# Four pieces for one: splitting GpSimd's 128x2048 subtractions in a three-layer transformer kernel

## The chip, the cores and the metric

The kernel runs on one NeuronCore of a Trainium2 chip. Its time is the device time of one execution in microseconds. The engines have one queue of instructions each: TensorE (PE in the profile, PEld for its weight loads), VectorE (DVE), ScalarE (ACT), GpSimd (POOL) and SyncE (SP, which here issues most of the loads). They wait for one another by semaphores.

## The reference

Three layers work on one sequence of 256 tokens with 1024 features, all in float32:

```
layers 0, 1:  h = rms_norm(x) * (1 + sc1) + sh1          # sh, sc, g from silu(c) @ ada_w
              x = x + g1 * attention(h @ w_qkv) @ w_o    # layer 0 differential, layer 1 banded with a relative bias
              h = rms_norm(x) * (1 + sc2) + sh2
              x = x + g2 * moe(h)                        # 16 experts, two per token
layer 2:      the same frame; p = h @ w_in feeds a gated mlp, attention over tokens and context,
              and a two-way gated scan; then @ w_out and an moe with 32 experts, two per token
```

## The kernel before, in words

Tokens lie in two tiles of 128 partitions (`NT = 2`). The dense weights (`w_qkv`, `w_o`, `w_in`, `w_out`) come in slabs of 128 partitions x 4 x 512 float32, 1 MB each, through `stream` (L231). SP loads a slab `w` (L243). `split` (L246) makes two float32r tiles of it: `hi`, a rounded copy (`copy`, L250 by way of L188, mostly on ACT), and `lo = w - hi` (`tt`, L251 by way of L199). The second is the operation at issue. A table (`ENG`, entries `sv0` and `sv1`, L142 and L143) and a default say whether it runs on DVE or GpSimd: 30 of these subtractions are on GpSimd, 16 on DVE.

`mm3` (L265) then multiplies in three passes: rounded activations by `hi`, the activations' low part by `hi`, and rounded activations by `lo`. So a slab's `lo` is wanted 16 matmuls later than its `hi`. `trans_split` (L482 to L199) makes the activations' own two parts at the start of a layer: `affine` on ACT (L519) and DVE (L521), and a 128x512 subtraction on DVE (L199).

All slabs, loads and large activations share one pool of 17 buffers named `u`. SP issues loads in program order and waits in the queue until the buffer is free; a slab is free when its subtraction has read it.

Small DVE work that stands beside the subtractions: `rsqrt` (L284), a chain of tiny operations, each needing the one before (L288, L289, then three times L295 or L297 and L298, and L299), for the norms of a layer (results used at L464) and of the queries and keys (used at L199, and then by TensorE's transposes at L573); `coef` (L452), the eight numbers per partition with which the layer's activations are scaled; and `ada_close` (L422), which ends a modulation vector.

The order of the steps in a mix stage is a string (`MIX_ORDER`), and the framework's scheduler sets the order within each engine's queue when the program is built. Between the mix stages stand the experts' stages (L1646 to L1716), whose weights are used unsplit; they have a 128x512 subtraction of their own on GpSimd (L1682). Before each expert stage all engines meet at a branch (L1725, L1726).

Of the kernel before, what the change touches and what calls it, by code (L numbers as in the profile page):

```python
# [9 lines left out]
F32 = mybir.dt.float32  # L10
# [3 lines left out]
OP = mybir.AluOpType  # L14
# [106 lines left out]
SPV = 3  # L121
# [44 lines left out]
class Gen:  # L166
# [64 lines left out]
    def stream(self, srcs, raw):  # L231


        srcs, loaded, ready = list(srcs), [], []
        n = [0]

        def load(m):
            while srcs and len(loaded) < m:
                src = srcs.pop(0)
                w = self.t("u", [128, 4, 512])  # L240
                n_ = 4 // len(src)
                for i, q in enumerate(src):
                    self.nc.sync.dma_start(w[:, i * n_:(i + 1) * n_], q)  # L243
                loaded.append(w)

        def split():  # L246
            w = loaded.pop(0)
            hi, lo = (self.t("u", list(w.shape), F32R) for _ in range(2))

            self.copy("sh", hi, w)  # L250
            self.tt("sv", lo, w, hi.bitcast(F32), OP.subtract, "VG" if n[0] % SPV == SPV - 1 else "GV")  # L251
            n[0] += 1
            ready.append((hi, lo))

        def get():
            load(raw)
            while loaded and len(ready) < 2:
                split()
                load(raw)
            return ready.pop(0)  # L260

        get.load, get.split = load, split
        return get
# [1625 lines left out]
```

## Time and profile before

| | |
|---|---|
| three runs | 1600.05, 1605.42, 1606.1 us; median 1605.42 |
| the profiled execution | 1605.76 us, of which 1603.9 us from its first to its last instruction |
| PE busy | 1448.1 us (90%), 7202 matmuls |
| DVE busy | 642.9 us (40%) |
| ACT busy | 405.2 us (25%) |
| POOL busy | 255.8 us (16%), 126 instructions |
| mean granted TensorE clock | 0.956 of full speed |
| HBM | 336 GB/s over the span |

The shares are averages over stages of two kinds. In the experts' stages the DMA engines are busy throughout (most slices at 410 to 423 GB/s in the page's strip) and GpSimd is nearly idle. The mix stages, at about 30 to 215, 440 to 660 and 900 to 1140 us, hold all the 128x2048 subtractions. There the DMA share is lower in most slices, and DVE's digit reaches 9.

### The profile page before, as it was taken

Reading aid. Unit: us, or ns where it says so; the run is one execution under the profiler, and the core shown is the slowest. Engines: PE = TensorE matmul, PEld = TensorE weight load, DVE = VectorE, ACT = ScalarE, POOL = GpSimd, SP = SyncE. Lnnn points to the kernel's source line nnn. Section 1 sums busy time; section 2 is a strip of 40 time slices with the busy share of each in tenths; the row PEclk is TensorE's granted clock in tenths of the full one; section 3 lists DMA queues with packets and bytes.
Section 4 is the critical chain, followed back from the end, with each engine's and each line's share of the span. In section 5 each row is a group of like instructions: output and inputs, shape, how many; then the busy total and the mean of one; then the engine's idle time right before and its main releaser. Section 6 shows DMA issues by size and latency. Waiting matters only on the chain. (4 is left out here: it accounts for less than half of the span.)

```text
span 1603.9 us, 18619 instructions
## 1 busy us (share of the span) xinstructions
PE 1448.1 (90%) x7202; PEld 768.5 (48%) x7202; DVE 642.9 (40%) x1404; ACT 405.2 (25%) x717; POOL 255.8 (16%) x126
## 2 busy tenths in 40 slices
PE   4999989999979988899999798678899999999997
PEld 1666643454356566444534265456435445434432
DVE  3678521221176675242122458976113122212212
ACT  1455211011054443132111255532111111101100
POOL 1332201101032412001000233321010100100100
PEclk8999979999989989999999899889899999999999
DMA  9787859999979937499999657318699999999997
GB/s 363 276 319 272 331 215 423 421 421 421 410 282 364 340 132 314 175 416 416 421 418 416 226 189 261 130 46 322 245 421 421 421 421 421 421 422 420 421 421 294
DMA packets 131071, 540.86 MB, mean 337 GB/s; under 512 B 8600, under 2 KB 13856, under 8 KB 83360
## 3 DMA queue, kind: packets, MB, share of 16 engines
q1 hardware_dynamic: 128032, 533.73, 83.9%
q10 hardware_dynamic: 2320, 3.89, 0.7%
q0 software_dynamic: 624, 1.98, 0.3%
q8 instruction: 60, 0.98, 0.2%
q14 instruction: 35, 0.29, 0.0%
HBM read 538.49 MB, written 1.06 MB: 336 GB/s over the span
## 5 line engine op out<-in xcount | busy, mean ns | idle before, releaser
L1646 PE MATMUL ps<-u,b 128*64 128x512 f32 x2048 | 487.9, 601 | 14.1 <-DMA u<-in_w_dram 10.2
L1646 PEld LDWEIGHTS ps<-u,b 128*64 128x64 f32 x2048 | 166.3, 138 | 303.7 <-issue 279.9
L270 PE MATMUL ps<-u 128*128 128x512 f32 x1104 | 278.4, 402 | 11.2 <-ACT u L188 4.8
L270 PEld LDWEIGHTS ps<-u 128*128 128x128 f32 x1104 | 203.7, 190 | 83.2 <-issue 24.1
L1675 PE MATMUL ps<-u,b 128*64 128x512 f32 x1024 | 232.5, 597 | 5.0 <-ACT b L1664 2.4
L1682 POOL TENSOR_TENSOR b<-b,b 128x512 fp32r<-128x512 f32 x58 | 78.1, 1362 | 811.6 <-ACT b L1681 713.9
L199 POOL TENSOR_TENSOR u<-u 128x2048 fp32r<-128x2048 f32 x30 | 144.0, 4809 | 273.2 <-ACT u L188 221.1
L1716 DVE TENSOR_TENSOR x<-x,ps 128x512 f32<-128x512 f32 x128 | 79.8, 682 | 210.1 <-PE ps L1710 210.1
L1675 PEld LDWEIGHTS ps<-u,b 128*64 128x64 f32 x1024 | 83.2, 136 | 126.1 <-issue 115.2
L1680 DVE SCALAR_TENSOR_TENSOR b<-ps,tiny,G 128x512 f32<-128x512 f32 x64 | 48.1, 751 | 183.9 <-PE ps L1675 175.4
L1653 DVE TENSOR_TENSOR b<-b,ps 128x512 f32<-128x512 f32 x32 | 22.0, 688 | 226.1 <-PE ps L1646 134.1
L415 PE MATMUL ps<-u,z 128*32 128x512 f32 x576 | 89.6, 656 | 15.9 <-DVE z L384 13.2
L1681 ACT CAST b<-b 128x512 fp32r<-128x512 f32 x64 | 39.3, 618 | 208.7 <-DVE b L1680 208.7
L1664 ACT COPY b<-ps 128x512 f32<-128x512 f32 x32 | 18.8, 586 | 274.2 <-PE ps L1662 274.2
L188 ACT CAST u<-u 128x2048 fp32r<-128x2048 f32 x44 | 82.7, 1911 | 15.3 <-DMA u<-in_a_w_qkv_dram 15.3
L1564 PE MATMUL ps<-b,u 128*128 128x512 f32 x256 | 78.2, 453 | 3.1 <-DVE b L1550 3.1
L1564 PEld LDWEIGHTS ps<-b,u 128*128 128x128 f32 x256 | 67.2, 329 | 20.3 <-issue 13.5
L1710 PE MATMUL ps<-b,b 128*128 128x512 f32 x256 | 70.2, 410 | 3.3 <-DVE b L1682 1.9
L1651 ACT ACTIVATE b<-ps 128x512 f32<-128x512 f32 x32 | 19.1, 597 | 194.1 <-PE ps L1646 194.1
L1710 PEld LDWEIGHTS ps<-b,b 128*128 128x128 f32 x256 | 45.2, 188 | 41.8 <-ACT b L1651 16.2
L521 DVE TENSOR_SCALAR b<-ps,mA,mod 128x512 f32<-128x512 f32 x32 | 25.9, 810 | 67.6 <-PE ps L1564 67.6
L519 ACT ACTIVATE b<-ps,mod,mA 128x512 f32<-128x512 f32 x32 | 24.9, 779 | 110.6 <-PE ps L1564 110.6
(347 smaller groups left out, 1295.0 us busy)
## 6 DMA issues: line engine op xcount, KB each, us to landing
u<-in_w_dram SPq DMA_DIRECT2D x192, 1024.0 KB, 19.8
u<-in_moe_w_gate_dram SPq DMA_DIRECT2D x64, 1024.0 KB, 11.5
u<-in_moe_w_up_dram SPq DMA_DIRECT2D x64, 1024.0 KB, 12.5
u<-in_moe_w_down_dram SPq DMA_DIRECT2D x64, 1024.0 KB, 12.7
u<-in_ada_w_dram SPq DMA_DIRECT2D x48, 1024.0 KB, 9.7
u<-in_w_mod_dram SPq DMA_DIRECT2D x24, 1024.0 KB, 7.7
u<-in_w_in_dram SPq DMA_DIRECT2D x14, 1024.0 KB, 5.6
u<-in_a_w_qkv_dram SPq DMA_DIRECT2D x12, 1024.0 KB, 13.8
```

Of the source, the lines that this page charges most:

```text
L188: (e.copy if e is self.nc.scalar else e.tensor_copy)(out, in_)
L199: self.pick(site, options).tensor_tensor(out, a, b, op=op)
L270: self.nc.tensor.matmul(p, x[a][:, k, t * 128:(t + 1) * 128], w[b][:, k % 4], start=start and i == 0 and k == ks[0], stop=stop and i == 2 ...
L415: self.nc.tensor.matmul(st["R"][32 * j:32 * j + 32, :], z[:, k, 11 - i:43 - i], w[:, k, :], start=(n == 0 and k < 4), stop=(last and k >= ...
L1564: nc.tensor.matmul(p, q[:, t, k:D:KC], P[:, t], start=(t == 0 and i == 0), stop=(t == 1 and i == 1))
L1646: nc.tensor.matmul(p[s * 64:(s + 1) * 64, :], hs[k // 2][:, k % 2, c0 + s * 64:c0 + (s + 1) * 64], W[e0, nm, k // 4, s][:, k % 4, :], star ...
L1675: nc.tensor.matmul(po[n][s * 64:(s + 1) * 64, :], heT[:, k, s * 64:(s + 1) * 64], w(s), start=(k == 0), stop=(k == 3), skip_group_check=True)
L1680: V.scalar_tensor_tensor(o, po[n], gs, g2[:, n * 512:(n + 1) * 512], op0=OP.mult, op1=OP.mult)
L1681: A.copy(oh[:, n], o)
L1682: (G if more else V).tensor_tensor(ol[:, n], o, oh[:, n].bitcast(F32), op=OP.subtract)
L1710: ins = nc.tensor.matmul(p, PT[:, t * 128:(t + 1) * 128], o[:, n, :], start=(i == 0), stop=(i == len(ops) - 1))
L1716: nc.vector.tensor_add(xs, xs, p)
```

## The change

Where a slab's subtraction falls to GpSimd, it is written as four instructions, one for each of the four 512-column blocks of the slab. On DVE it stays one instruction. `pick` is called as before, so the same 30 slabs go to GpSimd.

```diff
             self.copy("sh", hi, w)
-            self.tt("sv", lo, w, hi.bitcast(F32), OP.subtract, "VG" if n[0] % SPV == SPV - 1 else "GV")
+            e = self.pick("sv", "VG" if n[0] % SPV == SPV - 1 else "GV")
+
+            m = 4 if e is self.nc.gpsimd else 1
+            for j in range(m):
+                c = slice(4 // m * j, 4 // m * (j + 1))
+                e.tensor_tensor(lo[:, c], w[:, c], hi[:, c].bitcast(F32), op=OP.subtract)
             n[0] += 1
```

Lines behind it move down by five, and the subtraction is recorded at its own line, L256, instead of the helper's L199. GpSimd's queue at the start of layer 0, before (`u` are slabs, written as lo<-w,hi and numbered in the order of their making; the memset belongs to an attention bias):

```order
L199 TENSOR_TENSOR u_247<-u_242,u_246 128x2048 [waits DMAHW4_49,Activation_49]
L199 TENSOR_TENSOR u_251<-u_244,u_250 128x2048 [waits DMAHW5_49,DVE_49]
L594 MEMSET u_416 64x8x64 [waits DMAHW4_49,Pool_49]
L199 TENSOR_TENSOR u_420<-u_316,u_419 128x2048 [waits PE_49,DMAHW0_49,Activation_49,Pool_49]
L199 TENSOR_TENSOR u_452<-u_390,u_451 128x2048 [waits DMAHW3_49,PE_49,Activation_49]
```

The same place after the change:

```order
L256 TENSOR_TENSOR u_247<-u_242,u_246 128x512 [waits DMAHW4_49,Activation_49]
L256 TENSOR_TENSOR u_247<-u_242,u_246 128x512 x3
L256 TENSOR_TENSOR u_254<-u_244,u_253 128x512 [waits DMAHW5_49,DVE_49]
L256 TENSOR_TENSOR u_254<-u_244,u_253 128x512 x3
L599 MEMSET u_422 64x8x64 [waits DMAHW4_49,Pool_49]
L256 TENSOR_TENSOR u_426<-u_322,u_425 128x512 [waits PE_49,DMAHW0_49,Activation_49,Pool_49]
L256 TENSOR_TENSOR u_426<-u_322,u_425 128x512 x3
```

Four instructions stand where one stood, and only the first of the four waits (in a slab that two DMAs load, the third waits too). TensorE's queue at the same place, the second and third pass over the first slab, before (`u_246` is the slab's `hi` and `u_247` its `lo`, so the last three rows are the third pass; `ps` are the two token tiles):

```order
L270 MATMUL ps_282<-u_246,u_257 128x512 [waits DVE_49]
L270 MATMUL ps_282<-u_246,u_257 128x512
L270 MATMUL ps_283<-u_246,u_257 128x512 x2
L270 MATMUL ps_282<-u_246,u_257 128x512 [waits DVE_49]
L270 MATMUL ps_282<-u_246,u_257 128x512
L270 MATMUL ps_283<-u_246,u_257 128x512 x2
L270 MATMUL ps_282<-u_247,u_256 128x512 [waits Pool_49]
L270 MATMUL ps_282<-u_247,u_256 128x512 x3
L270 MATMUL ps_283<-u_247,u_256 128x512 x4
```

And after:

```order
L275 MATMUL ps_288<-u_246,u_263 128x512 [waits DVE_49]
L275 MATMUL ps_288<-u_246,u_263 128x512
L275 MATMUL ps_289<-u_246,u_263 128x512 x2
L275 MATMUL ps_288<-u_246,u_263 128x512 [waits DVE_49]
L275 MATMUL ps_288<-u_246,u_263 128x512
L275 MATMUL ps_289<-u_246,u_263 128x512 x2
L275 MATMUL ps_288<-u_247,u_262 128x512 [waits Pool_49] x4
L275 MATMUL ps_289<-u_247,u_262 128x512 x4
```

Each of the first four matmuls of the third pass now waits for its own piece, where the first alone waited for the whole. No instruction of TensorE, DVE, ACT or SP changes its place in its queue anywhere in the program.

## Rows read from the trace of the kernel before

**Rows 1.** Groups on POOL: operation, shapes, count | busy us, mean ns | idle before

```profile
L199 POOL TENSOR_TENSOR u<-u 128x2048 fp32r<-128x2048 f32 x30 | 144.0, 4809 | 273.2 <-ACT u L188 221.1 <-DVE b L196 24.2 <-issue 19.5
L1682 POOL TENSOR_TENSOR b<-b,b 128x512 fp32r<-128x512 f32 x58 | 78.1, 1362 | 811.6 <-ACT b L1681 713.9 <-DMA u<-in_moe_w_down_dram 51.5 <-DMA u<-in_w_dram 46.0
```

**Rows 2.** Timeline of POOL: start us, us, instruction; x2 is two in a row

```profile
340.55 2.50 POOL L1682 TENSOR_TENSOR b<-b,b 128x512 fp32r<-128x512 f32 x2 [31.66 <-ACT b L1681]
```

**Rows 3.** Timeline at the start of layer 0, 30 to 58 us

```profile
34.54 4.50 POOL L199 TENSOR_TENSOR u<-u 128x2048 fp32r<-128x2048 f32 x1 [14.29 <-ACT u L188]
35.70 3.37 DVE L452 SCALAR_TENSOR_TENSOR tiny<-mod,cst 128x8 f32<-128x8 f32 x1
...
39.78 3.56 PE L270 MATMUL ps<-u 128*128 128x512 f32 x8 [4.35 <-ACT u L519]
...
41.60 3.78 DVE L199 TENSOR_TENSOR u<-b,u 128x512 fp32r<-128x512 f32 x1
...
45.43 11.17 PE L270 MATMUL ps<-u 128*128 128x512 f32 x40 [2.08 <-DVE u L199]
```

**Rows 4.** Timeline in layer 0, 84 to 88 us

```profile
80.40 4.55 DVE L297 TENSOR_TENSOR tiny<-tiny 128x16 f32<-128x16 f32 x1
...
86.25 1.45 PE L573 MATMUL ps<-identR,b 128*128 128x128 f32 x8 [2.48 <-DVE b L199]
```

**Rows 5.** Timeline in layer 1, 554 to 568 us

```profile
555.53 10.06 POOL L199 TENSOR_TENSOR u<-u 128x2048 fp32r<-128x2048 f32 x2 [3.84 <-issue]
...
556.65 4.52 DVE L298 SCALAR_TENSOR_TENSOR tiny<-tiny 128x16 f32<-128x16 f32 x1
561.21 4.42 DVE L299 SCALAR_TENSOR_TENSOR tiny<-tiny 128x16 f32<-128x16 f32 x1
...
565.66 1.29 DVE L199 TENSOR_TENSOR b<-b,tiny 128x512 f32<-128x512 f32 x2
...
566.50 1.09 PE L573 MATMUL ps<-identR,b 128*128 128x128 f32 x4 [7.98 <-DVE b L199]
```

**Rows 6.** Busy us by engine in a stretch, PEclk, DMA share, GB/s

```profile
566.00:576.00 10.00, 9.51 (x39) 7.07 (x39) 5.97 (x17) 2.08 (x9) 0.27 (x1) 0.54 0.57 211
```

**Rows 7.** Timeline at the start of layer 2, 895 to 945 us

```profile
914.93 8.98 POOL L199 TENSOR_TENSOR u<-u 128x2048 fp32r<-128x2048 f32 x2 [31.01 <-ACT u L188]
...
915.14 4.34 DVE L295 SCALAR_TENSOR_TENSOR tiny<-tiny 128x1 f32<-128x1 f32 x1
...
919.40 0.15 DVE L452 SCALAR_TENSOR_TENSOR tiny<-mod,cst 128x8 f32<-128x8 f32 x1
919.51 4.42 DVE L299 SCALAR_TENSOR_TENSOR tiny<-tiny 128x1 f32<-128x1 f32 x1
...
924.86 0.75 DVE L464 TENSOR_SCALAR u<-x,tiny 128x1024 f32<-128x1024 f32 x1
```

**Rows 8.** Timeline in layer 2, 1046 to 1062 us

```profile
1047.49 5.39 POOL L199 TENSOR_TENSOR u<-u 128x2048 fp32r<-128x2048 f32 x1 [4.00 <-ACT u L188]
...
1049.69 3.75 DVE L199 TENSOR_TENSOR b<-b,u 128x512 f32<-128x512 f32 x1 [0.25 <-ACT b L1219]
...
1054.22 1.40 DVE L422 TENSOR_TENSOR b<-b,b 32x512 f32<-32x512 f32 x1
...
1055.76 2.11 PE L430 MATMUL ps<-cst,b 128*64 128x12 f32 x32 [5.92 <-DVE b L422]
```

**Rows 9.** Timeline of DVE in layer 2, 900 to 1062 us

```profile
1003.53 4.82 DVE L199 TENSOR_TENSOR b<-u 128x256 f32<-128x256 f32 x1
...
1033.05 4.02 DVE L1303 SCALAR_TENSOR_TENSOR b<-b,b 128x256 f32<-128x256 f32 x1
```

**Rows 10.** Waits of SP's queue, the two on POOL: us in total, times, longest

```profile
SPq L227 <- POOL u L199: 32.5, 5, 9.9
...
SPq L243 <- POOL u L199: 28.3, 6, 7.4
```

**Rows 11.** Line 199, who waited for it: us, times

```profile
  PEld ps L270: 3.3, 2
```

## The prediction

> **What bounds the kernel now.** I read the page first, for where the 128x2048 subtractions stand: all 30 are in the three mix stages, which end in a branch that every engine waits for, so a mix stage that ends earlier moves all that follows. Then I read the groups of GpSimd's instructions, for the price of a piece; the timeline of the mix stages, place by place, for what DVE does while GpSimd subtracts; and the waits, for who stands on GpSimd itself.
>
> GpSimd does not bound by its own time: TensorE's weight loads waited for line 199 on GpSimd for 3.3 us in two cases [rows 11]. The `lo` of a slab is wanted 16 matmuls after its `hi`, and it is nearly always there. What the timeline shows instead is that GpSimd's subtraction holds up DVE. A DVE operation on 128x16 numbers, 8 KB in all, that meets a subtraction lasts 4.5 us and ends when the subtraction ends [rows 4, 5]; one on 128x8 takes 0.15 us when it meets none [rows 7] and 3.37 us when it does [rows 3]. The held operations in these rows read two operands from SBUF. So DVE and GpSimd share something that one instruction holds to its end, and TensorE feels it through DVE: it stood for 4.35 and 2.08 us at the start of layer 0 [rows 3], 2.48 us in layer 0 [rows 4], 7.98 us in layer 1 [rows 5] and 5.92 us in layer 2 [rows 8].
>
> The rule that decides the case is what happens at the seam between two GpSimd instructions. Two pairs show it. In layer 1 DVE's L298 was held by the first subtraction, ended at 561.17, and L299 behind it was held by the second, to 565.63 [rows 5]. In layer 2 L295 got through at the seam at 919.48, L452 beside it, and L299 was held until the second ended [rows 7]. So a waiting DVE operation passes at a seam, and the one that depends on it is held by the next GpSimd instruction. I work with one held operation for each seam.
>
> **The price of a piece.** Two 128x512 subtractions in a row take 2.50 us [rows 2], 1.25 each, so four take 5.0 against 4.50 for one undisturbed 128x2048 [rows 3]: 0.5 us more, 15 us over 30, all on an engine with idle time before its groups [rows 1]. The group's mean of 1362 ns [rows 1] holds waiting as well, so it bounds the piece from above: 5.4 us for four.
>
> **The places, one by one.** Gains and losses are at TensorE or at the DVE work that holds it.
>
> Start of layer 0. The subtraction starts at 34.54, so the first seam is at 35.79, where L452 passes and ends near 35.95 instead of 39.07. TensorE began 0.71 us after that end (39.78), so now at 36.65: 3.1 us earlier. Its next wait, for L199 held 3.78 us until 45.38, moves too: behind L452 stand a cast of the second slab (counted as held too: second seam, 37.04), two operations that read PSUM, and this L199 at the third or fourth seam (39.5 to 40.8), so it ends 4 to 5 us earlier. Bounds -5.2 and -3.1; I take -4.0, since TensorE then meets the later pieces of `lo`.
>
> Layer 0, 80 us. The chain behind L297 is L297, L298, L299, then L199. Each takes a seam: 80.40 + 4 x 1.25 + some 0.4 of their own = 85.8, then 0.7 for L199, so that TensorE's transposes start near 86.65 and not at 86.25: +0.4.
>
> Layer 1, 555 us. The pair starts in earnest when DVE's own subtraction ends, at 555.53 + 10.06 - 9.0 = 556.6. L298 passes at the first seam, L299 at the second, the first L199 at the third (556.6 + 3.75 + 0.35 = 560.7) and ends at 561.4; the transposes start at 561.5, not 566.50. The second L199 passes one seam later and ends at 563.3, not 566.95, and the copy behind it waits for that: -3.7 to -5.0, taken as -4.2. Behind the long wait TensorE was granted 0.54 of full speed, mostly the lower of its two levels (1.2 of 2.4 GHz), for 10 us in which it was busy 9.51 [rows 6]; with 3 us of waiting in place of 8, part of that stretch may run at the upper level. Bounds 0 and -4.4 (9.51 x 0.46); I take -1.0, nearer to zero as DVE paces the softmax behind it.
>
> Start of layer 2, 915 us. Seven operations that depend on each other must pass before TensorE gets its input: L295, L299, L295, L299, L295, L299, and L464, which I count as held too. The seventh seam is at 914.93 + 7 x 1.25 = 923.7, against 924.86 now: -1.2. The like chain at the start of layer 1 meets one subtraction, and four seams pass four operations by the time the whole one ended: 0.
>
> Layer 2, 1047 us. The subtraction holds the pair from 1052.88 - 4.50 = 1048.4. L199 at 1049.69 passes at the second seam (1050.9) and ends at 1051.6, not 1053.44; L422 follows at the third seam and ends at 1053.4, not 1055.62. TensorE's wait of 5.92 us ends 2.2 us earlier: -2.2.
>
> Layer 2, 998 to 1045 us. DVE has no idle time there and nearly all of its operations are of the held kind. At 1003.53 it sees a pair: ten microseconds of pieces in place of nine, so it ends 0.5 us later; at 1033.05 four operations behind the held one read PSUM and run beside the next pieces, and it ends 0.5 us earlier [rows 9]. Sum 0.
>
> Loads. Eleven loads on SP's queue stood on a subtraction's end, for a buffer [rows 10]. Each is issued at least 0.5 us later: from 0 to 5.5 us, and I take +1.0, as transfers queued before them cover most.
>
> Everywhere else a DVE chain is held while TensorE has other matmuls; the chains end within 0.5 us of where they do now. TensorE's 90 added semaphore waits are for pieces long done and cost nothing; if a piece were late, TensorE's queue behind it would stand by up to 1.25 us, and the modulation matmuls with it.
>
> The sum: -4.0 + 0.4 - 4.2 - 1.0 - 1.2 - 2.2 + 0 + 1.0 = -11.2. The profiled execution took 1605.76 us (span 1603.9 and 1.86 around it), so 1594.6; the median of the runs lies 0.34 lower, so **1594.2 us**.
>
> The Trainium skill ("SBUF — State Buffer", section "Who interferes with whom") says that DVE with two SBUF inputs and a reading GpSimd instruction take turns at one pair of ports, and that whichever starts first keeps it for the whole instruction while the other fully blocks. The trace agrees: 4.42 us for a 128x16 operation. By that rule alone a split makes turns shorter but their sum longer, which speaks against this change wherever DVE has only such work; that is the second rival.
>
> **The rivals.**
>
> No hand-over (slower). If GpSimd's next piece is queued and takes the port at the seam before DVE does, every held operation waits for 5.0 us instead of 4.5, and every load stands 0.5 us longer. Were all 30 extra halves exposed, that is +15: 1620. It decides from 16 of 30 exposed on (8 us), say 20: 1615. For it: at a seam both are ready. Against it: both pairs above, where DVE passed.
>
> Gains given back (no change). DVE is released early but meets the next piece, and its next result is no earlier; only the two places where TensorE waits through one or two operations gain, layer 1 and 1047 us, half of their 6.4 us: 1602. For it: at 1003 us the sum is zero or worse, and in the chains a seam passes just one operation. Against it: the branches at the ends of the mix stages wait for exactly these chains.
>
> More passes (faster still). If several operations pass at each seam, a chain of tiny ones is over after two or three pieces: start of layer 0 -5.2, layer 0 0, layer 1 -9 with the clock, start of layer 2 -4.9 (free at 919.9, after the fourth seam), 1047 us -2.2: -21, or 1584. For it: L452 and L295 passed at one seam. Against it: L299 did not.
>
> **How the numbers follow.** Chances: forecast 0.45, given back 0.32, more passes 0.15, no hand-over 0.08. Three runs of before span 6 us, so 0.5% (8 us) is about what can be told from no change. Faster than 1597.4: 0.38 of the forecast's, all 0.15 and 0.03 of the given back: 0.56. Slower than 1613.4: 0.06 of no hand-over and 0.02 of others: 0.08. The same: 0.36. The range runs from 1585, just above the most that I can work out, to 1606, no gain at all.
>
> **What would show it.** In the profile after: 120 subtractions of 128x512 near 1.25 us; DVE's L452 at the start of layer 0 under 0.5 us; L298 and L299 in layer 1 at 1.3 us each where they were 4.5; TensorE's wait at that place near 3 us; its wait in layer 2 before L430 near 3.7. I am wrong if held operations still last 4.5 us or more, if TensorE's transposes at 566 do not move against the stage's start, or if the mix stages shorten by less than half of the sum.

## The result: 1584.52 us, where 1594.2 was predicted

The changed kernel took 1584.52 us in the median of five runs (1582.53 to 1590.49), before beside it 1605.38 us (1600.05 to 1606.10): a ratio of 0.9891, 95% interval [0.9874, 0.9909]. A second set gave 1582.85 us against 1601.36 us, 0.9883 [0.9861, 0.9905]. The gain is 18 to 21 us, where I had 11.2. The sign and the mechanism were right, the size was not, and the time lies half a microsecond below the range.

The profile after. The first row is GpSimd's group that answers to the first of [rows 1] (line numbers below line 251 are five higher than before; columns: busy us, mean ns, idle before):

```profile
L256 POOL TENSOR_TENSOR u<-u 128x512 fp32r<-128x512 f32 x120 | 166.0, 1417 | 251.4 <-ACT u L188 228.9
```

144.0 us of GpSimd's time became 166.0, 22 more, and yet the kernel is faster. The timeline of the start of layer 0 (start us, us, engine, instruction; in brackets the idle time before it and who ended that), which answers to [rows 3]:

```profile
34.62 12.85 POOL L256 TENSOR_TENSOR u<-u 128x512 fp32r<-128x512 f32 x8 [14.22 <-ACT u L188]
34.89 1.00 DVE L457 SCALAR_TENSOR_TENSOR tiny<-mod,cst 128x8 f32<-128x8 f32 x1
35.82 1.21 DVE L188 CAST u<-u 128x2048 fp32r<-128x2048 f32 x1
...
36.61 11.57 PE L275 MATMUL ps<-u 128*128 128x512 f32 x39 [1.98 <-ACT u L524]
```

The held operation ends at 35.89, at the first seam, not at 39.07; TensorE starts at 36.61 and no longer stops a second time for 2.08 us. The eight pieces take 12.85 us, not 10, because DVE now gets in between: its cast of 1.21 us, which goes through at the first seam right behind L457, and its own subtractions hold a piece in their turn.

Layer 1 at the place of [rows 5]. L303 and L304 are the former L298 and L299:

```profile
544.03 8.15 POOL L256 TENSOR_TENSOR u<-u 128x512 fp32r<-128x512 f32 x5 [3.56 <-DMA u<-in_b_w_o_dram]
...
545.14 1.26 DVE L303 SCALAR_TENSOR_TENSOR tiny<-tiny 128x16 f32<-128x16 f32 x1
546.44 1.20 DVE L304 SCALAR_TENSOR_TENSOR tiny<-tiny 128x16 f32<-128x16 f32 x1
547.67 3.38 DVE L199 TENSOR_TENSOR b<-b,tiny 128x512 f32<-128x512 f32 x2
549.52 0.63 PE L578 MATMUL ps<-identR,b 128*128 128x128 f32 x4 [2.51 <-DVE b L199]
```

4.52 and 4.42 us became 1.26 and 1.20, and TensorE's wait 7.98 became 2.51.

Layer 2, the chain of [rows 7], and the wait of [rows 8]. First the line of before with TensorE's wait for that chain, then the profile after:

```profile
925.67 1.97 PE L482 MATMUL ps<-identR,u 128*128 128x128 f32 x8 [6.95 <-DVE u L464]
```

```profile
900.19 10.29 POOL L256 TENSOR_TENSOR u<-u 128x512 fp32r<-128x512 f32 x8 [30.99 <-ACT u L188]
...
900.40 1.09 DVE L300 SCALAR_TENSOR_TENSOR tiny<-tiny 128x1 f32<-128x1 f32 x1
901.41 0.15 DVE L457 SCALAR_TENSOR_TENSOR tiny<-mod,cst 128x8 f32<-128x8 f32 x1
901.52 1.19 DVE L304 SCALAR_TENSOR_TENSOR tiny<-tiny 128x1 f32<-128x1 f32 x1
...
902.75 1.18 DVE L300 SCALAR_TENSOR_TENSOR tiny<-tiny 128x1 f32<-128x1 f32 x1
903.97 1.19 DVE L304 SCALAR_TENSOR_TENSOR tiny<-tiny 128x1 f32<-128x1 f32 x1
...
909.40 1.97 PE L487 MATMUL ps<-identR,u 128*128 128x128 f32 x8 [5.42 <-DVE u L469]
...
1035.89 2.10 PE L435 MATMUL ps<-cst,b 128*64 128x12 f32 x32 [3.98 <-DVE b L427]
```

This is the rule of the seam in the open: six operations of 128 numbers, 0.16 to 0.22 us of work each, leave one by one at 1.2 us, the length of a piece. L457, which needs none of their results, goes through beside the first of them. TensorE's wait fell from 6.95 to 5.42 us there, and from 5.92 to 3.98 before L435.

So the waits of TensorE that the prediction named moved the way it said. Two things were not in it. One stands in layer 2, further on. The other is the clock, which had only a small term, in layer 1: it is 0.956 in the profiled execution of before and 0.962 in that of after.

### The profile page after: what moved, and what is told of

It is laid out like the page before. It is cut to its first block, busy times and chain, and to the rows that moved or that the text cites. A ratio compares the mean times of both kernels' runs of the same rounds, so it can differ in the third digit from the quotient of the medians.

```text
span 1582.6 us, 18722 instructions
## 1 busy us (share of the span) xinstructions
PE 1443.0 (91%) x7202; PEld 769.3 (49%) x7202; DVE 629.3 (40%) x1404; ACT 404.9 (26%) x717; POOL 278.2 (18%) x216
## 3 DMA queue, kind: packets, MB, share of 16 engines
q0 software_dynamic: 624, 1.98, 0.3%
## 5 line engine op out<-in xcount | busy, mean ns | idle before, releaser
L1651 PEld LDWEIGHTS ps<-u,b 128*64 128x64 f32 x2048 | 166.0, 138 | 302.4 <-issue 278.9
L275 PE MATMUL ps<-u 128*128 128x512 f32 x1104 | 278.7, 403 | 3.4 <-ACT u L524 2.0
L275 PEld LDWEIGHTS ps<-u 128*128 128x128 f32 x1104 | 204.4, 191 | 75.0 <-issue 22.9
L256 POOL TENSOR_TENSOR u<-u 128x512 fp32r<-128x512 f32 x120 | 166.0, 1417 | 251.4 <-ACT u L188 228.9
L1680 PEld LDWEIGHTS ps<-u,b 128*64 128x64 f32 x1024 | 83.4, 136 | 125.9 <-issue 115.0
L1715 PEld LDWEIGHTS ps<-b,b 128*128 128x128 f32 x256 | 45.2, 188 | 41.8 <-ACT b L1656 16.2
```

The source lines that it names most:

```text
L256: e.tensor_tensor(lo[:, c], w[:, c], hi[:, c].bitcast(F32), op=OP.subtract)
L275: self.nc.tensor.matmul(p, x[a][:, k, t * 128:(t + 1) * 128], w[b][:, k % 4], start=start and i == 0 and k == ks[0], stop=stop and i == 2 ...
L1651: nc.tensor.matmul(p[s * 64:(s + 1) * 64, :], hs[k // 2][:, k % 2, c0 + s * 64:c0 + (s + 1) * 64], W[e0, nm, k // 4, s][:, k % 4, :], star ...
L1680: nc.tensor.matmul(po[n][s * 64:(s + 1) * 64, :], heT[:, k, s * 64:(s + 1) * 64], w(s), start=(k == 0), stop=(k == 3), skip_group_check=True)
L1715: ins = nc.tensor.matmul(p, PT[:, t * 128:(t + 1) * 128], o[:, n, :], start=(i == 0), stop=(i == len(ops) - 1))
```

## The experiments

**How the runs are compared.** One kernel's time varies with TensorE's granted clock: 62 runs of before, beside the experiments, go from 1598.88 us at 0.961 to 1607.39 at 0.952. I fitted the times of all kernels with one slope for all and a level for each: -0.83 us for each 0.001 of clock, and 1.2 us of scatter around it. The column "at 0.960" is a kernel's level less that of before. It takes out what the clock did, by chance or because of the change; the ratio does not.

| kernel | median us | ratio to before, 95% | mean clock | at 0.960 |
|---|---|---|---|---|
| changed kernel, two sets | 1584.52, 1582.85 | 0.9891, 0.9883 (above) | 0.9616 | -16.0, -15.9 |
| before, again | 1601.32 | 0.9988 [0.9978, 0.9997] | 0.9602 | -0.1 |
| pieces in layer 0 | 1595.60 | 0.9956 [0.9943, 0.9969] | 0.9615 | -4.5 |
| pieces in layer 1 | 1601.85 | 0.9983 [0.9968, 0.9999] | 0.9572 | -4.5 |
| pieces in layer 2 | 1596.55 | 0.9955 [0.9938, 0.9972] | 0.9577 | -7.3 |
| three slabs of layer 2 | 1598.33 | 0.9976 [0.9961, 0.9991] | 0.9584 | -4.2 |
| pieces by columns | 1588.03 | 0.9882 [0.9861, 0.9902] | 0.9604 | -15.5 |
| two pieces | 1596.65 | 0.9949 [0.9935, 0.9962] | 0.9586 | -7.1 |
| eight pieces | 1568.65 | 0.9772 [0.9758, 0.9785] | 0.9714 | -24 |
| sixteen pieces | 1580.46 | 0.9849 [0.9835, 0.9864] | 0.9690 | -13 |
| eight, four at first | 1568.12 | 0.9789 [0.977, 0.9808] | 0.9692 | -26 |
| sixteen, eight and four | 1560.91 | 0.9737 [0.9716, 0.9758] | 0.9726 | -30 |

The last four ran at clocks that before never reached (0.963 at most), so their last column is an extrapolation; their ratios stand by themselves.

The profiles give a check that needs no fit: TensorE's idle time, which is the span less TensorE's busy time. It is 155.8 and 154.2 us in the two profiled executions of before, 139.6 and 140.5 in those of the changed kernel, and 128.2, 139.1, 128.2 and 125.9 in the last four, in the order of the table. Between the first profile of before and that of after, 16.2 us are idle time and 5.1 are busy time (1448.1 and 1443.0 us).

The edits below are to the line `m = 4 if e is self.nc.gpsimd else 1` of the changed kernel, unless something else is shown.

**Before once more.** No edit.

> The kernel before, run once more, for its times against the granted clock of each run. Theory A (the gain beyond the forecast is clock: half-speed stretches that the shorter waits take away): the runs of before lie on one line against the clock, some 1.1 to 1.5 us for each 0.001, and at the clock of 0.956 they are 13 to 16 us above the changed kernel's run at 0.956 (1590.49); at their highest clock they don't come below 1598. Theory B (the clock differs by chance from run to run, and the change has no part in it): some runs of before show 0.960 or more and come near 1598 to 1600.

Measured: twelve runs with clocks from 0.954 to 0.963, 1606.46 down to 1599.84 us. Theory A had the distance right and the slope too steep (1.1 to 1.5 us for each 0.001, against 0.83). Theory B holds in part: the clock of one and the same kernel differs from run to run, by up to 8 us of time. But at no clock does before come near the changed kernel, whose slowest runs, 1590.49 and 1590.26 at 0.956, lie 14 to 15 us below the runs of before at that clock (1604.06 to 1605.72). In the pair of profiled executions 5 us of the 21 are this difference (0.006 at 0.83 us for 0.001), and 16 are not, as the busy and the idle time say.

**One layer at a time.**

```diff
+            m = 4 if e is self.nc.gpsimd and self.l == 0 else 1    # and == 1, == 2 in the others
```

> Pieces in layer 0 alone; layers 1 and 2 keep whole subtractions. Forecast's own terms (-4.0 + 0.4): 1601.8. Theory A (waits as forecast, and half-speed stretches behind them gone in layer 0, about -7): 1595, with no half-speed stretch near 46, 87 and 149 us. Theory C (more passes at a seam, without the clock): 1600.

> Pieces in layer 1 alone. Forecast's own terms (-4.2 and -1.0 of clock): 1600.2. Theory A, from the two traces (the wait at 566 us shorter by 5.4, the clock behind it no better): 1601.5. Theory C (start of layer 1 gains too): 1596.4.

> Pieces in layer 2 alone. Forecast's own terms (-1.2 - 2.2): 1602.0. Theory A, from the two traces (those two, 3.4 at TensorE's waits for the cast at 976 and 985, 2.2 at 1040, some of it given back to the clock): 1599.5. Theory C (start -4.9, 1047 us -2.2): 1598.3.

Measured at one clock: -4.5, -4.5, -7.3. Their sum, -16.3, is the changed kernel's -16.0 within the scatter, so the gains of the layers add up. Layer 0 and layer 1 are close to my terms without the clock (-3.6 and -4.2). Layer 2 gave 7.3 where I had 3.4: here lie the missing 4 us. On layer 0, theory A's time was met (1595.60 in the median, 1595 expected), but only half of its reason: 4.5 of the 7.3 us are there at a common clock, and the rest comes with a mean clock of 0.9615. Of the three half-speed stretches that it named (in before each lowers the clock of ten microseconds to 0.83), the one near 46 us is gone in every profile in which layer 0 has two or four pieces; the one near 87 us is gone in one profile of the changed kernel and there in the other; and the one near 149 us is missing as well from the profiles of two kernels that left layer 0 as it was. So the first goes with the shorter wait, and the last comes and goes by itself. The kernel with pieces in layer 1 shows why a median can mislead: seven of its runs stand at 1601.3 to 1603.3 (clock 0.953 to 0.956) and five at 1593.8 to 1598.8 (0.960 to 0.962).

**Three slabs of layer 2**, which the prediction had passed over:

```diff
+            m = 4 if e is self.nc.gpsimd and self.l == 2 and n[0] in (6, 7, 12) else 1
```

> Four pieces for three subtractions of layer 2 alone, those at 961, 976 and 1032 us in the trace of before; all others whole. Theory A, from the kernel with layer 2 alone (its gain of 7.3 at one clock, less the start's 1.5 and 1.5 at 1047): 4.5 below before at one clock, TensorE's wait at 976 us for the cast 0.6 instead of 2.3, that at 985 gone. The forecast (the chains off the listed places end within 0.5 us of where they did): no difference.

Measured: -4.2, as theory A had it. First the timeline of before (its run above, "Before once more"), then of this kernel, at the same work (L840 is L835, L842 is L837, L275 is L270):

```profile
961.27 4.90 POOL L199 TENSOR_TENSOR u<-u 128x2048 fp32r<-128x2048 f32 x1 [12.32 <-ACT u L188]
961.63 5.62 DVE L835 SCALAR_TENSOR_TENSOR u<-u 128x1024 f32<-128x1024 f32 x1
967.33 1.28 ACT L837 ACT_TABLE_LOAD   x1 [6.14 <-DVE u L835]
973.92 1.89 ACT L188 CAST u<-u 128x2048 fp32r<-128x2048 f32 x1
975.86 1.42 PE L270 MATMUL ps<-u 128*128 128x512 f32 x5 [2.33 <-ACT u L188]
981.22 1.28 ACT L1159 ACT_TABLE_LOAD   x1 [5.41 <-DVE u L849]
984.98 2.34 PE L270 MATMUL ps<-u 128*128 128x512 f32 x9 [1.72 <-ACT u L188]
```

```profile
958.64 7.34 POOL L256 TENSOR_TENSOR u<-u 128x512 fp32r<-128x512 f32 x4 [12.33 <-ACT u L188]
958.99 2.31 DVE L840 SCALAR_TENSOR_TENSOR u<-u 128x1024 f32<-128x1024 f32 x1
961.37 1.28 ACT L842 ACT_TABLE_LOAD   x1 [2.81 <-DVE u L840]
969.58 1.90 ACT L188 CAST u<-u 128x2048 fp32r<-128x2048 f32 x1
971.53 1.43 PE L275 MATMUL ps<-u 128*128 128x512 f32 x5 [0.64 <-ACT u L188]
974.62 1.28 ACT L1164 ACT_TABLE_LOAD   x1 [3.14 <-DVE u L854]
```

In before, TensorE waits for a cast on ScalarE, which seems to have nothing to do with GpSimd. But the cast stands on ScalarE's queue behind work that waited 6.14 us for DVE's L835, and L835 is held by the subtraction. With pieces that wait is 2.81, TensorE's first wait falls from 2.33 to 0.64 us, and the second (1.72) is gone. The third slab shortens TensorE's wait for DVE's L196 from 5.84 to 3.45 us. The changed kernel has the same. In the profile of before, and then in its own, the instruction reads:

```profile
1039.97 1.33 PE L1114 MATMUL ps<-identR,b 128*128 128x128 f32 x5 [5.89 <-DVE b L196]
```

```profile
1019.40 1.85 PE L1119 MATMUL ps<-identR,b 128*128 128x128 f32 x7 [3.68 <-DVE b L196]
```

That is 2.2 us at a place that I had put at nothing. The three waits of this kernel are 5.8 us shorter in all; two later ones are longer (0.7 us at 995 us, and 1.5 at 1058, where the subtraction is whole). That leaves 3.6 us, where the fit has 4.2.

**Pieces by columns**, to tell the seams from the other thing that four instructions bring, a first quarter of `lo` that is ready early:

```diff
-                c = slice(4 // m * j, 4 // m * (j + 1))
-                e.tensor_tensor(lo[:, c], w[:, c], hi[:, c].bitcast(F32), op=OP.subtract)
+                c = slice(512 // m * j, 512 // m * (j + 1))
+                e.tensor_tensor(lo[:, :, c], w[:, :, c], hi[:, :, c].bitcast(F32), op=OP.subtract)
```

> Four pieces as in the changed kernel, but each takes 128 of the 512 columns of all four k-slices, so that a matmul still waits for the last piece. Theory A (the gain is the seams, at which a held DVE operation passes): as the changed kernel, 14 to 18 us below before, DVE's first held operation at the start of layer 0 still near 1 us. Rival R (the gain is that TensorE's matmuls start on the first quarter of lo): nearly all of it gone, within 4 us of before.

Measured: -15.5 at one clock, against -16.0. The early quarter is worth nothing that can be measured; the gain is the seams. DVE's first held operation:

```profile
34.53 12.83 POOL L256 TENSOR_TENSOR u<-u 128x512 fp32r<-128x512 f32 x8 [14.35 <-ACT u L188]
34.80 1.01 DVE L457 SCALAR_TENSOR_TENSOR tiny<-mod,cst 128x8 f32<-128x8 f32 x1
```

**Two pieces, eight, sixteen.** In the last two a piece is a part of one k-slice.

```diff
+            m = 2 if e is self.nc.gpsimd else 1     # 8, 16 in the others, as lo[:, c, d] with d a part of 512
```

> Two pieces of 128x1024, some 2.3 us each. Theory A (one held operation for each seam): start of layer 0 -2.5, 566 us -2, start of layer 2 0 (seven operations for four seams), 961 us in layer 2 -1.5, 1033 us -1, 1047 us -1: 8 us below before at one clock. Rival C (several pass at a seam): the chains are over at the second seam, 13 us below before.

> Eight pieces of 128x256, some 0.7 us each by a line through 128x512 and 128x2048, 5.7 us in all. Theory A (one held operation for each seam): each held operation 0.6 us shorter than with four: against the changed kernel -1 at the start of layer 0, -1.6 at 80 us, -1.6 at the start of layer 1, -2 at 566 us, -3.8 at the start of layer 2, -0.5 at 1033, -1.3 at 1047, and +1 of later loads: 10 us below it. Rival C (several pass at a seam): the chains are over already; within 3 us of the changed kernel, or slower by later pieces.

> Sixteen pieces of 128x128, some 0.45 us each, 7 us for a slab. Theory A: held operations 0.25 us shorter than with eight, another -4; lo comes 1.3 us later than with eight, and eleven loads as well, +2: near the kernel with eight pieces, 2 us to either side. Rival C: slower than the changed kernel by 2 to 6 us.

Two pieces gave -7.1, where the rule of one operation for each seam said -8, and several passes -13. Their start of layer 2 settles it:

```profile
907.41 9.26 POOL L256 TENSOR_TENSOR u<-u 128x1024 fp32r<-128x1024 f32 x4 [30.99 <-ACT u L188]
...
907.62 2.18 DVE L300 SCALAR_TENSOR_TENSOR tiny<-tiny 128x1 f32<-128x1 f32 x1
909.83 2.27 DVE L304 SCALAR_TENSOR_TENSOR tiny<-tiny 128x1 f32<-128x1 f32 x1
912.13 2.26 DVE L300 SCALAR_TENSOR_TENSOR tiny<-tiny 128x1 f32<-128x1 f32 x1
914.42 2.26 DVE L304 SCALAR_TENSOR_TENSOR tiny<-tiny 128x1 f32<-128x1 f32 x1
916.72 0.22 DVE L300 SCALAR_TENSOR_TENSOR tiny<-tiny 128x1 f32<-128x1 f32 x1
```

Four seams let four operations out, and the fifth takes 0.22 us once GpSimd is done. "More passes", whose 1584 us the measurement met, is thereby refuted as a mechanism.

Eight pieces gave 16 us more than four in the median, more than the 10 expected. By the extrapolated fit 8 of them are there at one clock, by TensorE's idle time 11 (128.2 us against 139.6); the rest comes with a mean clock of 0.9714. Sixteen gave 12 of those 16 us back, where the two were expected within 2 us of each other. The trace tells where. In layer 0 TensorE waits 4.7 us for pieces of `lo` where it waited 1.7 with eight, 4.1 us for a DVE operation (L199) where it was 0.8, and 5.3 us for loads where it was 1.6. The last is a slab's buffer that comes free later: SP's queue stood 17.3 us on a subtraction, where the longest such wait of the stretch was 8.8 with eight, and issued the load at 81.90, and TensorE started when it had landed.

```profile
81.90 0.92 SPq L227 DMA_DIRECT2D u<-in_ada_w_dram  x2
...
87.91 1.05 PE L423 MATMUL ps<-u,z 128*32 128x512 f32 x2 [3.69 <-DMA u<-in_ada_w_dram]
```

TensorE did not wait for this load with eight. But eight pay as well, in layer 0, where TensorE meets late pieces of `lo`:

```profile
49.27 0.50 PE L278 MATMUL ps<-u 128*128 128x512 f32 x1 [0.86 <-POOL u L259]
50.64 1.78 PE L278 MATMUL ps<-u 128*128 128x512 f32 x4 [0.86 <-POOL u L259]
```

**Sizes by place.** Four pieces for the first two slabs of layer 0 and eight elsewhere; then also sixteen for the first two slabs of layers 1 and 2, where a tiny chain is all that TensorE waits for:

```diff
+            m = (4 if self.l == 0 and n[0] < 2 else 8) if e is self.nc.gpsimd else 1
+            m = ((16 if self.l else 4) if n[0] < 2 else 8) if e is self.nc.gpsimd else 1    # the second kernel
```

> Eight pieces as in the run before, but four for the first two slabs of layer 0, where eight let TensorE wait twice for 0.86 us on pieces of lo and cost 3.4 us against four by 55 us. Theory A: 3 us below the kernel with eight, near 1565.5. If those waits only move (the later pieces of lo are then what TensorE meets a little further on): 1568 to 1569.

> As the run before with eight pieces and four for the first two slabs of layer 0, but sixteen for the first two slabs of layers 1 and 2, where a chain of tiny DVE operations is all that TensorE waits for. Theory A (one held operation for each seam, so shorter pieces free the chain sooner, and lo is wanted late there): -1.6 at the start of layer 1 and -1.9 at the start of layer 2, as the kernel with sixteen showed against eight; 3.5 us below the run before, near 1564.5. Rival: what the start of a layer gains comes back when TensorE meets the last pieces of lo, 1.3 us later for each slab: 1567 to 1569.

The first gave 1568.12 us, no better in the median than eight throughout, so theory A's 3 us are not seen. The two waits of 0.86 us are gone from its trace, but TensorE's idle time is the same 128.2 us; the 2 us that the fit gives it are near what the scatter allows. The second gave 1560.91 us, 2.6% below before and the fastest of all, 7 us below the first where 3.5 were expected; between the two profiled executions, at 0.972 and 0.973, it is 3.8, and the rest goes with the mean clock (0.9726 against 0.9692). Its start of layer 2, where each link of the chain is now held for 0.38 us:

```profile
889.63 0.38 DVE L307 SCALAR_TENSOR_TENSOR tiny<-tiny 128x1 f32<-128x1 f32 x1
890.05 0.38 DVE L303 SCALAR_TENSOR_TENSOR tiny<-tiny 128x1 f32<-128x1 f32 x1
...
892.68 1.16 PE L490 MATMUL ps<-identR,u 128*128 128x128 f32 x8 [0.17 <-DVE u L472]
```

TensorE's wait there, 6.95 us in before and 5.42 with four pieces, is 0.17.

**The changed kernel once more.** No edit.

> The changed kernel once more, beside before on one chip. Theory A1 (the gain is 16 us of waits, and the granted clock of the two kernels differs by run and not by kernel): its mean clock within 0.001 of before's, 16 us between the medians. A2 (the shorter waits raise the clock as well, as with eight pieces): its mean clock 0.002 to 0.003 above before's, 18 us between the medians.

Measured: 18.5 us between the medians, and a mean clock of 0.9625; over both sets 0.9616 (11 runs, standard error 0.0009) against 0.9587 (0.0003) for 74 runs of before. That speaks for A2: about 2.4 us of the gain, at the fitted slope, come with a higher clock. What raises the clock stays open. With eight pieces TensorE idles for 128.2 us, and the clock is 0.013 above before's; but sixteen pieces leave TensorE idle as long as four do (139.1 and 139.6 us) at 0.9690 against 0.9616, and the kernels with pieces in layer 1 or 2 alone have shorter waits than before and no higher clock (0.9572 and 0.9577). No experiment held the waits fixed and changed the clock alone.

## Why the prediction was right in its mechanism, and where its size went

1. *A held DVE operation passes at a seam, one for each.* Right for operations that need each other's results, and shown at four sizes: 2.26, 1.19 and 0.38 us a step with two, four and sixteen pieces in place of 4.4. An operation that needs nothing from the held one can pass at the same seam, as the cast at 35.82 and L457 at 901.41 do.
2. *The price of a piece, 1.25 us.* Right for a piece alone. The group's mean of 1417 ns holds the pieces that DVE holds up in its turn: 22 us in sum where I had 15, and above the 1362 ns that I took as the bound.
3. *Start of layer 0, -4.0.* Waits 4.35 to 1.98 and 2.08 to none: -4.5. Held L452 was to be under 0.5 us; it is 1.00, because it began earlier against the seam; its end is where I put it. The cast behind it ended at 37.03 where I had 37.04, which is luck: I had it pass at the second seam, and it went through at the first and held GpSimd's second piece (the first two pieces took 3.56 us, not 2.5).
4. *80 us, +0.4.* TensorE's wait there went from 2.48 to this, +0.6:

```profile
80.44 1.23 PE L578 MATMUL ps<-identR,b 128*128 128x128 f32 x8 [3.05 <-DVE b L199]
```

5. *Layer 1 at 555 us, -4.2, and the start of layer 2, -1.2.* The first wait is 5.5 us shorter and a new one of 0.74 us follows it; layer 1 alone measured -4.5. At the start of layer 2 it is -1.5.
6. *1047 us, -2.2.* Measured -1.9.
7. *Loads, +1.0.* At most in part: one wait of TensorE for a load is new in layer 2, 0.59 us at 970.82 in the profile after and 0.34 in that of the second set. SP's queue waited for GpSimd as long as in [rows 10], 59.5 us in 12 waits against 60.8 in 11:

```profile
SPq L227 <- POOL u L256: 34.8, 5, 11.3
SPq L243 <- POOL u L256: 24.7, 7, 5.4
```

8. *"Everywhere else a DVE chain is held while TensorE has other matmuls; the chains end within 0.5 us of where they do now", and "Sum 0" for 998 to 1045 us.* This step failed. Three subtractions of layer 2, which it put at nothing, were worth 4.2 us. I had gone by the engine that TensorE's wait names; at 976 and 985 us that is ScalarE, and I did not follow ScalarE's own wait back to DVE. At 1040 us it was DVE itself, and I summed DVE's busy time instead of following the one chain that TensorE waits for.
9. *The clock, -1.0, and only in layer 1.* Too small and in the wrong place: some 2.4 us on average, and 5 in the pair of profiles, about half of that a matter of which execution was profiled. In layer 1 nothing came of it: behind the wait that became 2.51 us the clock granted over ten microseconds was 0.53, and 0.54 before.

The terms without the clock add up to -10.2; measured -16.0, and of the 5.8 between them 4.2 are step 8, 1.0 the term for the loads and 0.6 the rest. The rival "More passes" had 1584 us, half a microsecond from the measured time, but its mechanism is refuted by the chains above, so that is luck. The rival "No hand-over" is refuted by the rows above, in which each held link ends at the first seam. "Gains given back" happened in places, but for a small part of the gain: in the changed kernel the waits that stand at 995 and 1019 us in before are longer, 2.99 us where it was 2.36 and 8.34 where it was 7.73.

## What to carry to other kernels

Where a long GpSimd instruction reads SBUF beside chains of tiny DVE operations, its length is the latency of each link of the chain; cut it into pieces of the size that the chain can bear, short where only the chain is waited for, long where its own result or its buffer is wanted soon. When a wait names an engine that is innocent, follow that engine's own queue one step further back before calling a place covered. And compare runs at a common clock before giving a stage the credit for a few microseconds.

## What the runs showed of the hardware

Not all DVE operations are held. Beside the pieces a reduction of 128x512 numbers takes what it always takes, while a one-input operation on 128x16 numbers waits for the seam (DVE in layer 0 of the changed kernel, with GpSimd's pieces in the whole stretch):

```profile
64.76 0.69 DVE L561 TENSOR_REDUCE tiny<-b 128x8 f32<-128x512 f32 x1 [0.29 <-ACT b L560]
65.48 0.28 DVE L309 TENSOR_SCALAR tiny<-tiny 128x16 f32<-128x16 f32 x1
65.80 1.22 DVE L293 TENSOR_SCALAR tiny<-tiny 128x16 int32<-128x16 int32 x1
```

L293 takes 0.17 us when it meets nothing, so one input is no protection. The Trainium skill ("SBUF — State Buffer", section "Who interferes with whom") says that reductions never contend on this chip, and that a tensor_scalar can, in the modes that use both pairs of ports; the trace agrees, with 0.69 and 1.22 us. The runs show further that DVE gets its turn at a seam even when GpSimd's next instruction is ready (1.19 us a link beside pieces of 1.25). How many go through depends on what stands there. Of a chain in which each operation needs the one before, it is one. A free operation right behind went through too in two places (L457 of 0.15 us at 901.41, and the cast of 1.21 us at 35.82), while in layer 1 the second of two L199 operations on 128x512 numbers had to wait for the next seam (together 3.38 us where they took 1.29). What decides between these no run shows.

TensorE's granted clock differs from run to run of one program, 0.952 to 0.963 in before, worth 8 us of 1600. The Trainium skill ("TensorE: Matmul & The Clock Gate", section "Part 1: The HAM clock gate (the "warmup" mystery)") calls the number of slow matmuls variable from run to run; these times agree.
